# Token rows on ScalarE's DMA queue, token scales spread by a product, two parameter vectors loaded as compact rows

## The chip, the cores and the metric

One core of one Trainium2 chip runs the whole kernel as one launch. The metric is device time in microseconds (us) of one execution, as the median over several runs. TensorE does the matrix products, VectorE and ScalarE the element-wise work, GpSimd some of it too, and SyncE issues most of the transfers. In the profile these are PE (with PEld for its weight loads), DVE, ACT, POOL and SP; a "q" behind a name is the engine's instruction queue. A transfer is issued by an instruction on SP's, ACT's or POOL's queue and then runs on the core's 16 DMA engines.

## The reference, cut to what matters

2048 new tokens of one stream and 8 x 16 tokens of running streams go through one layer with shared weights. The model width is 1024.

```python
h = rmsnorm(x, norm1_g)                   # x * rsqrt(mean(x*x) + eps) * g
proj = h @ w_in                           # 1024 -> 3584
hq, hf, hi, hg, aq, ak, av = split(proj)
f = lb + (1 - lb) * sigmoid(hf)
o_h = hgrn2_scan(hq, 1 - f, hi, log(f))   # matrix state per head, chunked
o_h = rmsnorm(o_h, hg_norm_g) * silu(hg)
o_a = rmsnorm(band_attention(aq, ak, av), att_norm_g)
x = x + concat(o_h, o_a) @ w_out
x = x + relu(rmsnorm(x, norm2_g) @ w_up) ** 2 @ w_down
y = rmsnorm(x, final_norm_g)
```

The change concerns the first norm (its factor per token, here called the token scale), the norm weights `hg_norm_g` and the lower bound `lb`, which comes from `lb_param`.

## The kernel before

The 2176 tokens are 17 tiles of 128 (number 16 holds the running streams). Three phases follow one another: `phase_hgrn` (projections for the recurrence, woven with the scan), `phase_att` (projections for attention, woven with attention, and the output product) and `phase_mlp`. The first two go through the tiles in six groups, `GROUPS = [[0, 1, 16], [2, 3, 4], [5, 6, 7], [8, 9, 10], [11, 12, 13], [14, 15]]`. Every big product is three products of fp32r halves (`mm3`, L290 to L292): high times high, high times low, low times high.

**Weights.** `W` (L245 to L258) loads 512 KB pieces on SP's queue into `wraw`, which has two slots. ACT casts each to the high half (L256) and DVE subtracts to get the low half (L257), into slots for two weight blocks. A block of 256 columns serves all tiles of a group.

**Token tiles.** For each group an `HT` object makes the transposed, normed activations `hT_hi` and `hT_lo`. `load` (L175) fetches the transposed tile `xT` (512 KB, L182), multiplies it by the norm weights (L185), and gets `rb`, a 128x128 tile of token scales. `put` (L192) multiplies by the scales (L199) and splits into high and low (L201, L202). This is done for every tile twice: once in the first phase and once in the second, 34 times in all.

**Token scales.** `token_scale` (L205) fetches the tile's rows a second time, untransposed (512 KB on SP's queue, L210), into `x`, a buffer with one slot (`c.xst`). ACT squares and sums (L87), POOL turns the sum into the scale (L77, L79), and POOL's queue stores the 128 scales, 4 bytes each, in a DRAM tensor `rd` (L212). For all loads but the first three, `rb` is then read back with one DRAM row copied to all 128 partitions (L189, on SP's queue). For the first three tiles ACT spreads the scale along a row (L187) and PE turns it by a product with the identity (L197, tile `rT`).

**Small parameters.** `gain_tile` (L65) loads `hg_norm_g` as one DRAM row copied to 128 partitions (256 KB into SBUF, L68). `lower_bound` (L336) loads 512 single elements into a 128x4 tile (L343). The mask table `mf` (L588) uses the one slot of `c.xst` too.

**Order.** The program is written as generators that `weave` mixes by costs written into the code, and the token scales of the next group stand after the `f` projections of the group at hand (L405). The framework under the kernel then puts each engine's instructions in an order of its own, which is fixed before the run: an instruction that waits for nothing in that order's reckoning can stand far ahead of its place in the text. On the chip each engine and each queue works in that fixed order.

Of the kernel before, what the change touches and what calls it, by code (L numbers as in the profile page):

```python
# [8 lines left out]
F32 = mybir.dt.float32  # L9
# [3 lines left out]
AF = mybir.ActivationFunctionType  # L13
ALU = mybir.AluOpType
# [3 lines left out]
P = 128  # L18
D = 1024
KT = D // P  # L20
NPT = 16
NTT = 17
# [7 lines left out]
GROUPS = [[0, 1, 16], [2, 3, 4], [5, 6, 7], [8, 9, 10], [11, 12, 13], [14, 15]]  # L30
# [6 lines left out]
HN = KT * P * max(len(x) for x in GROUPS_M)  # L37
# [27 lines left out]
def gain_tile(c, pool, name, a):  # L65
    n = a.shape[-1]
    t = pool.tile([P, n], F32, name=name)
    c.nc.sync.dma_start(out=t, in_=a.broadcast_to([P, n]))  # L68
    return t


def rsq(c, ss, n, width, key="", r=None):
# [18 lines left out]
def rows(c, prompt, sample, t):  # L91
    return prompt[t * P:(t + 1) * P, :] if t < NPT else sample
# [56 lines left out]
class HT:  # L149
# [24 lines left out]

    def load(self, t):  # L175
        c, nc = self.c, self.c.nc
        first = t in GROUPS[0] and t not in c.r1_known
        rb = c.small.tile([P, P], F32, tag="rb", name="rb", bufs=3)
        if first:
            token_scale(c, t)  # L180
        xT = c.xin.tile([P, D], F32, tag="x", name="xT")
        nc.sync.dma_start(out=xT, in_=c.xT[t])  # L182
        xT = xT.rearrange("p (k t) -> p k t", k=KT)
        eng = nc.vector if first and t != NPT else nc.gpsimd
        eng.tensor_tensor(out=xT, in0=xT, in1=c.g1[:, :, None].broadcast_to([P, KT, P]), op=ALU.mult)  # L185
        if first:
            nc.scalar.activation(rb, c.ones, AF.Copy, scale=c.r1[:, t:t + 1])  # L187
        else:
            nc.sync.dma_start(out=rb, in_=c.rd[t:t + 1, :].broadcast_to([P, P]))  # L189
        return xT, rb, first  # L190

    def put(self, x, col):  # L192
        c, nc = self.c, self.c.nc
        xT, rb, first = x
        if first:
            ps = c.ps_tx.tile([P, 4, P], F32, tag=c.ps_tx_tag, name="rT")[:, 0, :]
            nc.tensor.matmul(ps, rb, c.ident, start=True, stop=True)  # L197
            rb = ps
        nc.vector.tensor_tensor(out=xT, in0=xT, in1=rb[:, None, :].broadcast_to([P, KT, P]), op=ALU.mult)  # L199
        h = self.hi[:, :, col]  # L200
        nc.scalar.copy(h, xT)  # L201
        nc.vector.tensor_tensor(out=self.lo[:, :, col], in0=xT, in1=h.bitcast(F32), op=ALU.subtract)  # L202


def token_scale(c, t):  # L205

    nc = c.nc
    c.r1_known.add(t)
    x = c.xst.tile([P, D], F32, tag="x", name="x")
    nc.sync.dma_start(out=x, in_=rows(c, c.x_prompt, c.x_sample, t))  # L210
    rsq(c, sumsq(c, x, D), 1, D, r=c.r1[:, t:t + 1])
    nc.gpsimd.dma_start(out=c.rd[t:t + 1, :].rearrange("o p -> p o"), in_=c.r1[:, t:t + 1])  # L212


class OT(HT):
# [111 lines left out]
def fm_cost(cs):  # L327
    return 0.01 * (cs.stop - cs.start) / PARTS
# [7 lines left out]
def lower_bound(c, pool):  # L336

    nc = c.nc
    a = pool.tile([P, 4], F32, name="lb_a")
    e = pool.tile([P, 4], F32, name="lb_e")  # L340
    c.lb = pool.tile([P, 4], F32, name="lb")
    c.lb1 = pool.tile([P, 4], F32, name="lb1")
    nc.sync.dma_start(out=a, in_=c.lb_param.rearrange("o (h p) -> p (o h)", p=P))  # L343
    mx = pool.tile([P, 4], F32, name="lb_m")
    nc.vector.tensor_copy(mx, a)
    nc.vector.tensor_tensor(out=a, in0=a, in1=mx, op=ALU.subtract)
    nc.scalar.activation(e, a, AF.Exp)
    nc.vector.reciprocal(a, e)
    nc.vector.tensor_tensor(out=e, in0=e, in1=a, op=ALU.mult)
    nc.vector.tensor_tensor(out=c.lb, in0=e, in1=e, op=ALU.subtract)  # L350
    nc.vector.tensor_scalar(out=c.lb1, in0=c.lb, scalar1=-1.0, scalar2=1.0, op0=ALU.mult, op1=ALU.add)


def hgrn_proj(c, gs, start):

    nc = c.nc
    hT = start
    GMAX = max(len(x) for x in GROUPS) * P
    flat = c.h0p.tile([P, HN], F32, tag="h_hi", name="qf")
    b = c.h0p.tile([P, HN], F32, tag="h_lo", name="bias")  # L360
    c.bias = b[:, :AH * 640].rearrange("p (h k) -> p h k", h=AH)
    c.oa = b[:, AH * 640:AH * 640 + D]
    for gi, g in enumerate(gs):
        tiles = GROUPS[gi]
        n = len(tiles) * P
        nxt = None
        g.v = [c.hv.tile([P, 512], F32, tag="v", name="v") for _ in tiles]

        def tok(w, dst, ch, sig, done, pre=None):
            for j in range(len(tiles)):  # L370
                if pre:
                    pre()
                for _, ps in proj_tm(c, w, hT, [j]):
                    if ps is None:
                        yield TM_COST
                        continue
                    d = dst[j][:, ch * WC:(ch + 1) * WC]
                    if sig:
                        sg = c.sig.tile([P, 512], F32, tag="sig", name="sig")[:, :WC]
                        nc.scalar.activation(sg, ps, AF.Sigmoid)  # L380
                        nc.gpsimd.tensor_tensor(out=sg, in0=sg, in1=c.hgain[:, ch * WC:(ch + 1) * WC], op=ALU.mult)
                        nc.vector.tensor_tensor(out=d, in0=ps, in1=sg, op=ALU.mult)  # L382
                    else:
                        nc.scalar.copy(d, ps)
                    yield TM_COST
                done.append(j)

        w = next(c.ws)
        yield from tok(w, g.v, 0, False, [], pre=hT.add)
        o = 4 * GMAX * (gi % 2)  # L390
        g.q, g.f = (flat[:, x:x + HGH * GMAX].rearrange("p (h n) -> p h n", h=HGH)[:, :, :n]
                    for x in (2 * o, 2 * o + HGH * GMAX))
        for ch in range(2):
            w = next(c.ws)
            for f, cs, ps in proj_fm(c, w, hT, n):
                if ps is None:
                    yield fm_cost(cs)
                    continue
                h = ch * 2 + f
                sg = c.sig.tile([P, 512], F32, tag="sig", name="sig")[:, :cs.stop - cs.start]  # L400
                nc.scalar.activation(sg, ps, AF.Sigmoid)  # L401
                nc.vector.tensor_scalar(out=g.f[:, h, cs], in0=sg, scalar1=c.lb1[:, h:h + 1],
                                        scalar2=c.lb[:, h:h + 1], op0=ALU.mult, op1=ALU.add)
                yield fm_cost(cs)
        for t in GROUPS[gi + 1] if gi + 1 < len(gs) else []:  # L405
            token_scale(c, t)
        if 1 <= gi <= 4:
            att_bias(c, 2 * gi - 2, 2)
        for ch in range(2):
            w = next(c.ws)  # L410
            for f, cs, ps in proj_fm(c, w, hT, n):
                if ps is None:
                    yield fm_cost(cs)
                    continue
                nc.scalar.copy(g.q[:, ch * 2 + f, cs], ps)
                yield fm_cost(cs)
        g.fq = True
        w = next(c.ws)
        yield from tok(w, g.v, 1, False, [])
        g.gate = [c.hv.tile([P, 512], F32, tag="gate", name="gate") for _ in tiles]  # L420
        for ch in range(2):
            w = next(c.ws)
            if ch:
                nxt = HT(c, GROUPS[(gi + 1) % len(gs)])
            fin = []
            for cost in tok(w, g.gate, ch, True, fin):
                if nxt and len(fin) > nxt.next:
                    nxt.add()
                    cost += 0.5
                yield cost  # L430
        g.ready = True
        hT = nxt
    yield from att_v(c, c.vt, GROUPS[0], hT)
    c.hT0 = hT
# [127 lines left out]
def phase_hgrn(c):  # L562
    tc, nc = c.tc, c.nc
    with ExitStack() as s:
        def pool(name, bufs, **k):
            return s.enter_context(tc.tile_pool(reuse_waits="tile", name=name, bufs=bufs, **k))
        cp = pool("h_const", 1)
# [9 lines left out]
        c.ps_o = pool("h_pso", 1, space=PSUM)  # L577
        c.ps_st = pool("h_psst", 1, space=PSUM)
        c.state = cp.tile([P, HGH, P], F32, name="state")
        hT = HT(c, GROUPS[0])  # L580
        hT.add()
        next(c.ws)
# [10 lines left out]
        c.qm = [cp.tile([P, 4 * 144], F32, name=f"qm{i}") for i in range(2)]  # L593
        for x in c.qm:
            nc.gpsimd.memset(x, 0.0)
        c.hgain = gain_tile(c, cp, "hgain", c.hg_g)
        gs = [Ctx() for _ in GROUPS]
        for g in gs:
            g.ready = g.fq = False
# [505 lines left out]
def hymba_kernel(ctx, tc, x_prompt, x_sample, state_hgrn, cache_k, cache_v, lb_param, norm1_g, w_in,  # L1105
# [3 lines left out]
    c = Ctx()  # L1109
# [11 lines left out]
    dram = pool("dram", 1, space=DRAM)  # L1121
    c.small = pool("small", 2)
    consts(c, const)
    c.og = dram.tile([NTT * P, D], F32, name="og") if dbg is None else dbg
    c.rd = dram.tile([NTT, P], F32, name="rd")
    c.x1 = dram.tile([NTT * P, D], F32, name="x1")
    c.sq, c.sk = (dram.tile([4, P, P], F32, name=x) for x in ("sq", "sk"))
    c.sv = dram.tile([P, 512], F32, name="sv")
# [7 lines left out]
    with ExitStack() as s:  # L1136
        c.vp0 = s.enter_context(tc.tile_pool(reuse_waits="tile", name="v0", bufs=3))
        hTp = s.enter_context(tc.tile_pool(reuse_waits="tile", name="hT", bufs=1))
        n = max(len(x) for x in GROUPS) * P
# [68 lines left out]
```

## Time and profile before

| what | value |
|---|---|
| time, median of 3 runs | 3036.85 us (3036.55 to 3037.67) |
| profiled execution, its own time | 3034.61 us |
| its span, first to last instruction | 3032.8 us |
| PE busy | 2904.2 us, 96% |
| DVE, ACT, POOL busy | 1746.6, 1103.7, 301.5 us |
| mean granted clock of TensorE | 0.984 |
| moved by DMA | 330.48 MB, mean 109 GB/s |

Busy time of PE is the time in which a matmul runs, at whatever clock was granted; a granted clock of 0.5 is 1.2 GHz and 1.0 is 2.4 GHz. The "chain that ended last" follows the work back from the last instruction to what released each step. A wait names the instruction that waited and the one that it was put down to.

### The profile page before, as it was taken

To read this page: it belongs to the slowest core of one execution; us is meant where nothing else is said; L and a number is where in the kernel's file an instruction comes from. 1 tells how busy PE (TensorE), PEld (TensorE's weight loads), DVE (VectorE), ACT (ScalarE), POOL (GpSimd) and SP (SyncE) were. 2 spreads that over 40 slices of the span, in tenths; PEclk is the share of its full clock that TensorE was granted. 3 is DMA by queue.
4 is the path that set the end of the run, shared out by engine and by line. 5 is a ranking of instruction groups with operands and counts; after the bars stand their busy time and mean duration, and the time that the engine had idled before them with its cause. 6 is when DMAs were issued, how large, how long until landed. Compare 5 with 4: busy or idle time off the path is not lost.

```text
span 3032.8 us, 47202 instructions
## 1 busy us (share of the span) xinstructions
PE 2904.2 (96%) x18902; PEld 2680.0 (88%) x18902; DVE 1746.6 (58%) x3114; ACT 1103.7 (36%) x2258; POOL 301.5 (10%) x509
## 2 busy tenths in 40 slices
PE   5789999999999999998999999999999999999998
PEld 5788999998889888988888899999999999899997
DVE  4357666675556565656555546555555555555555
ACT  3242343343544545454222323233322223322232
POOL 2221222222002020102000000000000000000000
PEclk8889999999999999999999999999999999999999
DMA  8764333343325243446532332233212122322221
GB/s 171 159 130 127 97 120 115 94 148 126 111 82 174 74 155 105 144 153 208 190 100 65 113 113 88 73 98 118 76 57 70 56 70 86 123 70 83 71 83 64
DMA packets 118796, 330.48 MB, mean 109 GB/s; under 512 B 14192, under 2 KB 42480, under 8 KB 118576
## 3 DMA queue, kind: packets, MB, share of 16 engines
q1 hardware_dynamic: 111712, 308.84, 34.0%
q0 software_dynamic: 6864, 18.63, 1.6%
q8 instruction: 148, 2.42, 0.3%
q14 instruction: 72, 0.59, 0.1%
HBM read 294.90 MB, written 32.51 MB: 108 GB/s over the span
## 4 chain that ended last, share of the span: by engine, by line
PE 81%; DMA 8%; DVE 4%; ACT 2%; issue 2%; POOL 2%; SPq 0%; ACTq 0%; POOLq 0%; DVEq 0%
PE mm L290 23%; PE mm L292 23%; PE mm L291 23%; PE ps_oT L708 3%; DMA x<-in_x_prompt 2%; PE S L679 2%; PE S L701 2%; PE ps_sc L472 2%; DMA wraw<-in_w_in 1%; DMA rd<-r 1%; ACT junk L87 1%; DVE wlo L257 1%; PE ps_sc L465 1%; PE tx L101 1%; DMA x<-x 1%
## 5 line engine op out<-in xcount | busy, mean ns | idle before, releaser
L256 ACT CAST whi<-wraw 128x512 fp32r<-128x512 f32 x816 | 497.5, 620 | 753.7 <-PE mm L292 560.8
L257 DVE TENSOR_TENSOR wlo<-wraw,whi 128x512 fp32r<-128x512 f32 x816 | 562.5, 705 | 241.8 <-ACT whi L256 238.3
L290 PE MATMUL mm<-h_hi,whi 128*128 128x384 f32 (+1 forms) x1536 | 503.2, 328 | 1.9 <-DVE h_lo L104 1.9
L292 PE MATMUL mm<-h_hi,wlo 128*128 128x384 f32 (+1 forms) x1536 | 501.4, 326 | 0.0
L291 PE MATMUL mm<-h_lo,whi 128*128 128x384 f32 (+1 forms) x1536 | 500.7, 326 | 0.0
L1081 DVE TENSOR_TENSOR y<-mm,y 128x512 f32<-128x512 f32 x544 | 373.3, 689 | 219.3 <-PE mm L292 217.6
L290 PE MATMUL mm<-whi,uh 128*128 128x512 f32 x1088 | 423.6, 389 | 2.4 <-ACT uh L1061 2.4
L292 PE MATMUL mm<-whi,ul 128*128 128x512 f32 x1088 | 424.3, 390 | 0.8 <-DVE ul L1062 0.7
L291 PE MATMUL mm<-wlo,uh 128*128 128x512 f32 x1088 | 424.0, 390 | 0.0
L290 PE MATMUL mm<-whi,hT_hi 128*128 128x256 f32 x1264 | 381.6, 302 | 42.5 <-DVE gate L382 16.2
L292 PE MATMUL mm<-whi,hT_lo 128*128 128x256 f32 x1264 | 371.5, 294 | 3.6 <-DVE hT_lo L104 2.2
L291 PE MATMUL mm<-wlo,hT_hi 128*128 128x256 f32 x1264 | 370.1, 293 | 0.0
L290 PEld LDWEIGHTS mm<-whi,hT_hi 128*128 128x128 f32 x1264 | 250.6, 198 | 55.5 <-DVE gate L382 17.7
L290 PEld LDWEIGHTS mm<-h_hi,whi 128*128 128x128 f32 x1536 | 288.4, 188 | 6.9 <-issue 3.5
L291 PEld LDWEIGHTS mm<-h_lo,whi 128*128 128x128 f32 x1536 | 288.4, 188 | 1.2
L292 PEld LDWEIGHTS mm<-h_hi,wlo 128*128 128x128 f32 x1536 | 288.4, 188 | 0.0
L290 PE MATMUL mm<-hT_hi,whi 128*128 128x384 f32 (+1 forms) x768 | 263.7, 343 | 19.8 <-ACT sig L401 13.4
L1059 DVE SCALAR_TENSOR_TENSOR u<-mm,u 128x384 f32<-128x384 f32 (+1 forms) x192 | 102.4, 533 | 279.3 <-ACT u L1058 279.3
L292 PEld LDWEIGHTS mm<-whi,hT_lo 128*128 128x128 f32 x1264 | 250.8, 198 | 8.6 <-DVE hT_lo L104 3.1
L291 PE MATMUL mm<-hT_lo,whi 128*128 128x384 f32 (+1 forms) x768 | 256.0, 333 | 0.0
L292 PE MATMUL mm<-hT_hi,wlo 128*128 128x384 f32 (+1 forms) x768 | 255.7, 333 | 0.0
L291 PEld LDWEIGHTS mm<-wlo,hT_hi 128*128 128x128 f32 x1264 | 251.1, 199 | 1.9 <-issue 1.4
(182 smaller groups left out, 4008.1 us busy)
## 6 DMA issues: line engine op xcount, KB each, us to landing
wraw<-in_w_in SPq DMA_DIRECT2D x168, 512.0 KB, 4.3
wraw<-in_w_up SPq DMA_DIRECT2D x96, 512.0 KB, 4.1
wraw<-in_w_down SPq DMA_DIRECT2D x96, 512.0 KB, 4.0
wraw<-in_w_out SPq DMA_DIRECT2D x48, 512.0 KB, 3.9
xT<-in_x_T SPq DMA_DIRECT2D x34, 512.0 KB, 4.5
og<-og SPq DMA_DIRECT2D x17, 512.0 KB, 4.0
x<-yo POOLq DMA_DIRECT2D x68, 128.0 KB, 3.3
x<-x SPq DMA_DIRECT2D x17, 512.0 KB, 5.1
```

Source lines behind the costliest of these rows:

```text
L87: nc.scalar.activation(junk[:, :n], x, AF.Square, accum_out=ss)
L256: nc.scalar.copy(hi, rw)
L257: nc.vector.tensor_tensor(out=lo, in0=rw, in1=hi.bitcast(F32), op=ALU.subtract)
L290: nc.tensor.matmul(ps, lh, rh, start=(i == 0), stop=False)
L291: nc.tensor.matmul(ps, lh, rl, start=False, stop=False)
L292: nc.tensor.matmul(ps, ll, rh, start=False, stop=(i == n - 1))
L472: nc.tensor.matmul(pc[:, h * n2:(h + 1) * n2, :], ks[:, h, :], up[:, h], start=True, stop=True)
L679: nc.tensor.matmul(S[:, bk, :n], a[es, qc], c.K[ft][es, b, kc], start=(a is q and not b), stop=(a is ql))
L701: nc.tensor.transpose(ps[:, x, :], s[:, x * P:(x + 1) * P], c.ident)
L708: nc.tensor.matmul(poT[64 * e:64 * e + 64, j, :], g.vt[i - nk + 1 + x][:, 64 * h:64 * h + 64], pts[e][:, x, :], start=(x == 0), stop=(x == ...
L1059: nc.vector.scalar_tensor_tensor(out=u2, in0=ps, scalar=0.0, in1=u2, op0=ALU.max, op1=ALU.mult)
L1081: nc.vector.tensor_tensor(out=ysl, in0=ps, in1=ysl, op=ALU.add)
```

## The change

The rows of a token tile for its scale are issued on ACT's queue instead of SP's. For group 0 all three tiles' rows are loaded at the very start, each into a part of its own of the large tile `qf` (`c.xfirst`). For later groups a generator, `token_scales`, is advanced at each finished `f` and `q` projection of the group before: one step computes the scale of the last tile loaded and issues the load of the next one. The scales stay in the SBUF tile `c.r1`: the store to `rd`, the tensor `rd` and the read back are gone, and every `load` makes `rb` with an ACT instruction and every `put` turns it with a product with the identity, as only the first three did. `hg_norm_g` is loaded as one 2 KB row and spread by a product with a row of ones and a copy from PSUM; `lb_param` is loaded as four rows of 512 bytes and transposed on PE.

```diff
+def gain_rows(c, t, a, ps_pool, tag):
+    nc = c.nc
+    n = a.shape[-1]
+    nc.sync.dma_start(out=t[0:1, :], in_=a)
+    def spread():
+        for o in range(0, n, 512):
+            ps = ps_pool.tile([P, 512], F32, tag=tag, name="grow_ps")
+            nc.tensor.matmul(ps, c.ones[0:1, :], t[0:1, o:o + 512], start=True, stop=True)
+            nc.scalar.copy(t[:, o:o + 512], ps)
+    return spread
...
     def load(self, t):
-        first = t in GROUPS[0] and t not in c.r1_known
-        rb = c.small.tile([P, P], F32, tag="rb", name="rb", bufs=3)
+        first = t not in c.r1_known
         if first:
-            token_scale(c, t)
+            token_scale(c, t, c.xfirst[t])
...
-        if first:
-            nc.scalar.activation(rb, c.ones, AF.Copy, scale=c.r1[:, t:t + 1])
-        else:
-            nc.sync.dma_start(out=rb, in_=c.rd[t:t + 1, :].broadcast_to([P, P]))
+        rb = c.small.tile([P, P], F32, tag="rb", name="rb", bufs=3)
+        nc.scalar.activation(rb, c.ones, AF.Copy, scale=c.r1[:, t:t + 1])
...
     def put(self, x, col):
-        if first:
-            ps = c.ps_tx.tile([P, 4, P], F32, tag=c.ps_tx_tag, name="rT")[:, 0, :]
-            nc.tensor.matmul(ps, rb, c.ident, start=True, stop=True)
-            rb = ps
-        nc.vector.tensor_tensor(out=xT, in0=xT, in1=rb[:, None, :].broadcast_to([P, KT, P]), op=ALU.mult)
+        ps = c.ps_tx.tile([P, 4, P], F32, tag=c.ps_tx_tag, name="rT")[:, 0, :]
+        nc.tensor.matmul(ps, rb, c.ident, start=True, stop=True)
+        nc.vector.tensor_tensor(out=xT, in0=xT, in1=ps[:, None, :].broadcast_to([P, KT, P]), op=ALU.mult)
...
-def token_scale(c, t):
+def token_scale(c, t, x):
     c.r1_known.add(t)
-    x = c.xst.tile([P, D], F32, tag="x", name="x")
-    nc.sync.dma_start(out=x, in_=rows(c, c.x_prompt, c.x_sample, t))
     rsq(c, sumsq(c, x, D), 1, D, r=c.r1[:, t:t + 1])
-    nc.gpsimd.dma_start(out=c.rd[t:t + 1, :].rearrange("o p -> p o"), in_=c.r1[:, t:t + 1])
+
+def token_scales(c, tiles):
+    x = None
+    for t in list(tiles) + [None]:
+        if x is not None:
+            token_scale(c, last, x)
+        if t is not None:
+            last, x = t, c.xst.tile([P, D], F32, tag="x", name="x")
+            c.nc.scalar.dma_start(out=x, in_=rows(c, c.x_prompt, c.x_sample, t))
+        yield
...
 def lower_bound(c, pool):
-    nc.sync.dma_start(out=a, in_=c.lb_param.rearrange("o (h p) -> p (o h)", p=P))
+    row = c.small.tile([P, P], F32, tag="rb", name="rb", bufs=3)[0:4, :]
+    nc.sync.dma_start(out=row, in_=c.lb_param.rearrange("o (h p) -> (o h) p", p=P))
+    ps = c.ps_tx.tile([P, 4, P], F32, tag=c.ps_tx_tag, name="lbT")[:, 0, :4]
+    nc.tensor.transpose(ps, row, c.ident[0:4, 0:4])
+    nc.vector.tensor_copy(a, ps)
...
 def hgrn_proj(c, gs, start):
-    flat = c.h0p.tile([P, HN], F32, tag="h_hi", name="qf")
+    flat = c.qf
...
+        scales = token_scales(c, GROUPS[gi + 1] if gi + 1 < len(gs) else [])
...
+                next(scales, None)      # after each f projection, and after each q projection
                 yield fm_cost(cs)
-        for t in GROUPS[gi + 1] if gi + 1 < len(gs) else []:
-            token_scale(c, t)
...
         g.fq = True
+        if not gi:
+            c.hgain_put()
...
 def phase_hgrn(c):
+        c.qf = c.h0p.tile([P, HN], F32, tag="h_hi", name="qf")
+        c.xfirst = {}
+        for j, t in enumerate(GROUPS[0]):
+            c.xfirst[t] = c.qf[:, j * D:(j + 1) * D]
+            nc.scalar.dma_start(out=c.xfirst[t], in_=rows(c, c.x_prompt, c.x_sample, t))
         hT = HT(c, GROUPS[0])
...
-        c.hgain = gain_tile(c, cp, "hgain", c.hg_g)
+        c.hgain = cp.tile([P, 512], F32, name="hgain")
+        c.hgain_put = gain_rows(c, c.hgain, c.hg_g, c.ps_tx, c.ps_tx_tag)
...
-    c.rd = dram.tile([NTT, P], F32, name="rd")
```

## Rows read from the trace of the kernel before

**Rows 1.** Windows of 100 us: busy time and instructions per engine, granted clock, DMA share, GB/s.
```profile
0.00:100.00 100.00, 59.40 (x294) 57.01 (x294) 37.17 (x52) 36.34 (x66) 28.33 (x54) 0.85 0.76 173
100.00:200.00 100.00, 74.88 (x507) 71.78 (x508) 51.57 (x95) 33.05 (x74) 26.00 (x41) 0.81 0.77 140
...
500.00:600.00 100.00, 99.50 (x771) 97.64 (x770) 64.50 (x130) 38.62 (x90) 25.43 (x39) 1.00 0.33 103
```

**Rows 2.** Instructions of PE by line and shape, 0 to 200 us.
```profile
L290 PE MATMUL mm<-whi,hT_hi 128*128 128x256 f32 x120 | 42.1, 351 | 28.3 <-DVE gate L382 10.5 <-ACT hT_hi L201 9.1 <-ACT qf L415 8.6
...
L290 PE MATMUL mm<-hT_hi,whi 128*128 128x384 f32 x88 | 33.4, 379 | 15.7 <-ACT sig L401 13.4 <-ACT v L384 2.3
```

**Rows 3.** Timeline of PE at either clock: start, duration, instruction.
```profile
14.78 0.41 PE L290 MATMUL mm<-whi,hT_hi 128*128 128x256 f32 x1
...
15.00 0.41 PE L291 MATMUL mm<-wlo,hT_hi 128*128 128x256 f32 x1
...
29.22 0.28 PE L292 MATMUL mm<-whi,hT_lo 128*128 128x256 f32 x1
...
29.34 0.28 PE L290 MATMUL mm<-whi,hT_hi 128*128 128x256 f32 x1
...
51.72 0.33 PE L292 MATMUL mm<-hT_hi,wlo 128*128 128x384 f32 x1
51.89 0.33 PE L290 MATMUL mm<-hT_hi,whi 128*128 128x384 f32 x1
```

**Rows 4.** Chain that ended last, 0 to 600 us: start, duration, what.
```profile
11.54 10.54 DMA x<-in_x_sample
...
49.99 11.57 DMA rd<-r
62.52 10.42 DMA wraw<-in_w_in
...
224.80 1.78 PE ps_sc L454 x16
```

**Rows 5.** Waits of SP's queue, 0 to 200 us: total, times, longest.
```profile
SPq L210 <- DMA x<-in_x_prompt: 46.1, 10, 8.5
...
SPq L189 <- DMA rd<-r: 37.1, 6, 10.8
```

**Rows 6.** Windows of 10 us, columns as in rows 1.
```profile
10.00:20.00 10.00, 6.21 (x26) 5.70 (x26) 6.85 (x7) 3.51 (x6) 3.43 (x4) 1.00 1.02 113
...
40.00:50.00 10.00, 10.00 (x60) 9.96 (x59) 4.10 (x6) 6.63 (x11) 4.14 (x7) 1.00 0.99 246
...
60.00:70.00 10.00, 4.56 (x19) 4.24 (x17) 2.66 (x3) 0.00 (x0) 0.00 (x0) 0.84 0.73 33
```

**Rows 7.** Waits of ACT, 0 to 200 us.
```profile
ACT junk L87 <- DMA x<-in_x_prompt: 63.2, 13, 12.1
```

**Rows 8.** Instructions on tile x, 0 to 200 us: count, duration (ns) min/median/max, first and last start.
```profile
L87 ACT ACTIVATE junk<-x x17: 1044/1057/1058, 4.8 to 171.5; 128x1024 bf16<-128x1024 f32 x17
L210 SPq DMA_DIRECT2D x<-in_x_prompt x16: 327/328/944, 1.2 to 163.0; - x16
...
DMA to landing us min/median/max: 3.7/8.3/11.2
```

**Rows 9.** DMA issues of the whole run: count, KB each, median us to landing.
```profile
xT<-in_x_T SPq DMA_DIRECT2D x34, 512.0 KB, 4.5
```

**Rows 10.** Read backs and the multiplication by scales, whole run, columns as in rows 8.
```profile
L189 SPq DMA_DIRECT2D rb<-rd x31: 319/327/1374, 52.8 to 1076.2; - x31
...
L199 DVE TENSOR_TENSOR xT<-xT,rb x31: 1207/1215/2918, 61.8 to 1221.5; 128x1024 f32<-128x1024 f32 x31
```

**Rows 11.** Timeline at the start: the first scale's product, the first projection product.
```profile
8.33 0.80 PE L197 MATMUL rT<-ident,rb 128*128 128x128 f32 x2 [8.33 <-ACT rb L187]
...
12.51 0.58 PE L290 MATMUL mm<-whi,hT_hi 128*128 128x256 f32 x1 [3.38 <-ACT hT_hi L201]
...
24.27 0.40 ACT L187 ACTIVATE rb<-ones,r 128x128 f32<-128x128 f32 x1
```

More of the change, by code (lines that the diff above doesn't have):

```diff
@@ L185, in load @@
         eng.tensor_tensor(out=xT, in0=xT, in1=c.g1[:, :, None].broadcast_to([P, KT, P]), op=ALU.mult)
-        if first:
-            nc.scalar.activation(rb, c.ones, AF.Copy, scale=c.r1[:, t:t + 1])
-        else:
-            nc.sync.dma_start(out=rb, in_=c.rd[t:t + 1, :].broadcast_to([P, P]))
-        return xT, rb, first
+        rb = c.small.tile([P, P], F32, tag="rb", name="rb", bufs=3)
+        nc.scalar.activation(rb, c.ones, AF.Copy, scale=c.r1[:, t:t + 1])
+        return xT, rb
     def put(self, x, col):
         c, nc = self.c, self.c.nc
-        xT, rb, first = x
-        if first:
-            ps = c.ps_tx.tile([P, 4, P], F32, tag=c.ps_tx_tag, name="rT")[:, 0, :]
-            nc.tensor.matmul(ps, rb, c.ident, start=True, stop=True)
-            rb = ps
-        nc.vector.tensor_tensor(out=xT, in0=xT, in1=rb[:, None, :].broadcast_to([P, KT, P]), op=ALU.mult)
+        xT, rb = x
+        ps = c.ps_tx.tile([P, 4, P], F32, tag=c.ps_tx_tag, name="rT")[:, 0, :]
+        nc.tensor.matmul(ps, rb, c.ident, start=True, stop=True)
+        nc.vector.tensor_tensor(out=xT, in0=xT, in1=ps[:, None, :].broadcast_to([P, KT, P]), op=ALU.mult)
         h = self.hi[:, :, col]
@@ L202, in put @@
         nc.vector.tensor_tensor(out=self.lo[:, :, col], in0=xT, in1=h.bitcast(F32), op=ALU.subtract)
-def token_scale(c, t):
-    nc = c.nc
+def token_scale(c, t, x):
     c.r1_known.add(t)
-    x = c.xst.tile([P, D], F32, tag="x", name="x")
-    nc.sync.dma_start(out=x, in_=rows(c, c.x_prompt, c.x_sample, t))
     rsq(c, sumsq(c, x, D), 1, D, r=c.r1[:, t:t + 1])
-    nc.gpsimd.dma_start(out=c.rd[t:t + 1, :].rearrange("o p -> p o"), in_=c.r1[:, t:t + 1])
+def token_scales(c, tiles):
[7 more added lines that the diff above has]
+        yield
 class OT(HT):
@@ L415, in hgrn_proj @@
                 nc.scalar.copy(g.q[:, ch * 2 + f, cs], ps)
+                next(scales, None)
                 yield fm_cost(cs)
         g.fq = True
+        if not gi:
+            c.hgain_put()
         w = next(c.ws)
```

## Prediction

> **What bounds the kernel now.** I first read the windows of busy time. From 500 us on PE is busy nearly all the time at full clock, with 99.5 of 100 us as the pattern [rows 1]; nothing but less work on PE makes that part shorter. The first 200 us are different: PE is busy for 59.4 and 74.9 us, so 65.7 us are idle, and the granted clock is 0.85 and 0.81 there [rows 1]. So I looked for what this change can win in those 200 us, and for what it costs on PE after them.
>
> How much work is in the 200 us? PE ran 801 instructions there (294 + 507) [rows 1]. By line and shape, 120 x 3 are projection products with 256 columns and 88 x 3 with 384 [rows 2]; the other 177 belong almost all to the scan. At full clock successive projection products start 0.12 us apart with 256 columns and 0.17 us with 384; at granted clock 0.5 the spacing for 256 is 0.22 [rows 3]. The scan's records cost 1.78/16 = 0.111 us each in a dense stretch [rows 4]. The work is then 360 x 0.12 + 264 x 0.17 + 177 x 0.111 = 43.2 + 44.9 + 19.6 = 107.7 us. The stage takes 200. Of the 92.3 us between, 65.7 are idle and 26.6 are busy time at the low clock.
>
> Next, what released the work. In the chain that ended last the early pieces are transfers, not products: 10.5 us for the third tile's rows, 11.6 us for the 512-byte store to `rd`, then 10.4 us for a weight piece that stood behind it [rows 4]; row after row load follows in it up to 162 us. The waits of SP's queue say why the weight piece was late: SP stood 37.1 us for the `rd` store to land before it could issue the read back (L189), and 46.1 us for the one slot of `x` (L210) [rows 5]; weight pieces are issued behind both. The windows of 10 us show that the DMA engines are not short of capacity: at 40 us they moved 246 GB/s, but at 10 us 113 and at 60 us 33 GB/s while their busy share was 1.02 and 0.73 [rows 6]. In the second of these `rb` read-backs were in flight, in the first `hgain` and `lb_a`: transfers that copy one row 128 times or take single elements fill the engines with little data.
>
> Last, ACT. It stood 63.2 us in 13 waits for an `x` tile [rows 7]. All 17 sums of squares ran between 4.8 and 171.5 us [rows 8], although the text has each group's behind projections of the group before: the framework moved them ahead. In that order ACT's casts and copies stand behind each of these waits, and PE behind them.
>
> **The change part by part.**
>
> *Start.* The rows of tiles 0, 1 and 16 are issued at once and need no slot. The first scale product starts at 8.3 us and the first projection product at 12.5 us [rows 11]; the three row loads share the DMA engines with `xT` and the first weights now, so I keep 12.5 us. The 10.5 us for tile 16's rows [rows 4] go, and `mf`, `hgain` and `lb` no longer stand in front of weights.
>
> *Store and read back.* 31 read-backs (L189) [rows 10] and 17 stores leave; with them SP's 37.1 us [rows 5] and the 11.6 + 10.4 us of the chain at 50 us [rows 4]. What is late next there is PE itself or ACT.
>
> *Row loads on ACT's queue.* SP's 46.1 us [rows 5] go. The load still needs the one slot, which ACT frees itself, so ACT's path for the 14 later tiles stays serial: issue, landing, sum. Issue is 0.33 and the sum 1.06 us [rows 8]. For the landing I have 8.3 us here as the median, among the slow transfers [rows 8], and 4.5 us as the whole run's median for a piece of the same size [rows 9]. So 14 tiles take between 14 x 5.9 = 82 and 14 x 9.7 = 136 us. I take 5.7 us, nearer to the lower end since the transfers that filled the engines are gone but weights and biases are denser: 14 x 7.1 = 99 us. Queued behind the waiting sum on ACT are casts, sigmoids and copies, and behind those PE.
>
> *How long the stage gets.* By PE alone: 11.7 us of start (12.5 less the 0.8 that PE was busy), 107.7 of work, and 5 us because the first busy us run at half clock as now (6.2 of them up to 20 us [rows 6], where the spacing, not the clock's column, shows it, and about 4 more before the spacing is 0.12 at 29.2 us [rows 3]; half of the 10 is lost): 124 us. By ACT: the first of the 14 loads can go at about 20 us (it goes at 30.7 now, and the chain there loses the 10.5 us), then 99, then the 28 us that the stage has behind its last sum (200 - 171.5): 147 us. ACT's path is the longer: 147 us, a gain of 53. With the two landings it is 130 or 184, a gain of 70 or 16. Later stages only shift, PE being full.
>
> Of the landing a rule of the Trainium skill speaks against the change. Transfers started by several engines run on the same 16 DMA engines and interleave; starting them from another queue saves only issue time (DMA: Bandwidth & Descriptors, section "Issuing engines are not separate DMA queues"). By it the new queue itself shortens no landing, and with 8.3 us the sum would be a gain of 16 for the stage instead of 53; the trace bears it out so far as it shows landings of 8.3 us in the crowd and 4.5 elsewhere, and cannot show two queues here, ACT issuing nothing now.
>
> *New work on PE.* 31 products with the identity come in. The nearest row of the same shape, 128x128 in fp32 as two records, is the scan's 2 x 0.111 = 0.22 us [rows 4]; alone and at half clock such a pair took 0.80 [rows 11]. In a dense stream the first holds: 31 x 0.22 = 6.9 us (upper bound 24.8). `hgain`'s spread has four times the columns in one product, 0.9 us. The transposed `lb` is below 0.22. All of it counts in full, for PE has no slack after 200 us: 8 us.
>
> *Costed at nothing.* 31 more ACT instructions of 0.40 us [rows 11], 12.4 us in all, hide in ACT's idle 60% (38.6 busy of 100 us in the dense stage [rows 1]); if a wait of ACT uncovers them they are 12.4 us. DVE reads the scales from PSUM instead of SBUF in the same instruction. In the second phase the product takes one of three PSUM banks of `mm` until DVE is done with it; at worst 17 x 1.2 us, the length of one multiplication [rows 10], 20 us. POOL loses 17 issues and was not the bound.
>
> *Sum.* Gain 53 - 8 = 45 us. The profiled execution took 3034.6 us (span 3032.8 and 1.8 around it): 2989.6. The median is 2.2 us above it: 2992.
>
> **The rivals.**
>
> *ACT's queue is where the wait goes (gain small).* The landing stays at 8.3 us: 16 - 8 = 8 us, 3029. For it: ACT's 63.2 us [rows 7] remain by construction, the slot still being one. Against it: the landings were long beside transfers that now leave [rows 6]. Chance 0.18, for 3012 to 3031. The rule of the Trainium skill named above would make this case.
>
> *The order changes in favour of PE (gain large).* The framework may leave the row loads further back, now that they cost ACT's time, or ACT's waits may fall under PE's work; then PE's path binds: 200 - 124 - 8 = 68, 2969. For it: two PSUM banks of products and two weight blocks stand between ACT and PE. Against it: they did not hide ACT's waits before. Chance 0.15.
>
> *Slower: PE itself waits for the scales.* Before, a late `rb` held DVE's L199; now it holds a product in PE's fixed order, and behind it the projections. Place: the 14 products of the later groups in the first phase. Price: ACT's mean wait for a tile, 63.2/13 = 4.9 us [rows 7], is what an `rb` behind such a wait is late: 14 x 4.9 = 68, so 45 - 68 = 23 us slower, 3060. It decides from 45/14 = 3.2 us per product. For it: PE's first product waited 8.3 us for exactly this [rows 11]. Against it: only group 1's three scales are computed near their use; the others are known long before. Chance 0.08.
>
> *Nothing changes* because another early wait (weights through two slots) takes over: 0.04.
>
> **How the numbers follow.** My forecast, 2992 with its own range of 2976 to 3012, has 0.55. The range of 2971 to 3028 takes in that, most of the small gain and about half of the large one. Under 0.2% (6 us) a change cannot be told from none here. Faster by more: 0.55 + 0.18 + 0.15 = 0.88; same 0.04; slower 0.08.
>
> **What would show it.** In the profile after, SP's waits for `rd` and `x` are gone and weight pieces follow one another in the first 150 us; PE's idle time in the first 200 us falls from 65.7 to about 25 and its granted clock rises; the last sum of squares comes at about 120 us instead of 171; ACT's waits for `x` stay near 14 with some 3 us each. PE's busy time of the `rT` product is about 8 us in all. I am wrong if landings on ACT's queue stay at 8 us, if `rT` shows long waits of PE, or if the sums of squares are no longer in the first 150 us.

## Result and the profile after

The changed kernel takes 3002.68 us (median of 4 runs, 2997.01 to 3009.67); the kernel before took 3036.95 beside it. The ratio is 0.9888 with a 95% interval of 0.9867 to 0.9909. The forecast was 2992 us with a range of 2971 to 3028. The time lies in the range and the direction is right; the gain is 34 us where 45 was forecast. What follows shows that the length of the first stage came out almost as worked out, in part by luck, and that the reason given for it was mostly the wrong one.

The windows of the kernel after, with the columns of [rows 1] and [rows 6]:

```profile
0.00:100.00 100.00, 79.42 (x528) 75.59 (x529) 59.06 (x96) 53.23 (x100) 31.44 (x62) 1.00 0.74 243
100.00:200.00 100.00, 94.66 (x680) 90.27 (x680) 63.75 (x124) 38.33 (x86) 19.49 (x27) 0.95 0.37 117
...
10.00:20.00 10.00, 3.24 (x9) 2.06 (x9) 7.37 (x9) 7.44 (x14) 4.30 (x5) 1.00 0.84 284
...
60.00:70.00 10.00, 10.00 (x61) 8.99 (x61) 2.58 (x4) 4.61 (x9) 0.84 (x3) 1.00 0.75 241
```

PE is idle for 200 - 79.4 - 94.7 = 25.9 us of the first 200 instead of 65.7 [rows 1], and the granted clock rose from 0.85 and 0.81 to 1.00 and 0.95. The two windows in which the DMA engines were busy with little data [rows 6] now move 284 and 241 GB/s, at busy shares of 0.84 and 0.75 (1.02 and 0.73 before).

Instructions on tile `x`, and the waits of ACT and SP's queue, 0 to 200 us, in the kernel after:

```profile
L228 ACTq DMA_DIRECT2D x<-in_x_prompt x14: 334/334/352, 25.0 to 105.7; - x14
L101 ACT ACTIVATE junk<-x x14: 1044/1057/1058, 30.8 to 112.7; 128x1024 bf16<-128x1024 f32 x14
...
DMA to landing us min/median/max: 3.5/4.5/8.0
```
```profile
ACT junk L101 <- DMA x<-in_x_prompt: 23.4, 13, 4.9
```
```profile
SPq L268 <- DVE wlo L274: 105.3, 32, 12.3
SPq L195 <- DVE hT_lo L211: 20.5, 5, 10.4
```

Rows land after 4.5 us instead of 8.3 [rows 8], the last sum of squares starts at 112.7 us instead of 171.5, ACT waits 23.4 us for rows instead of 63.2 [rows 7], and SP waits mostly for buffers that DVE frees and for 16.9 us behind weight loads; its waits for `rd` and `x` [rows 5] are gone.

A landmark gives the stage's gain: the first scan tile's output is issued at 199.07 us before and at 145.41 after, 53.7 us earlier (53 was forecast). One execution tells this only to some 5 us: a second profile of the changed kernel (E5) has 150.01 us. In the first profile the lead then shrinks: 42.6 us at the 17th scan tile (720.52 against 677.92), 38.2 at the 16th attention tile (1390.01 against 1351.79), 33.1 at the end of the span. So 21 us are given back, where the forecast had 8.

### The profile page after: what moved, and what is told of

It is laid out like the page before. It is cut to its first block, busy times and chain, and to the rows that moved or that the text cites. A ratio compares the mean times of both kernels' runs of the same rounds, so it can differ in the third digit from the quotient of the medians.

```text
span 2999.7 us, 47223 instructions
## 1 busy us (share of the span) xinstructions
PE 2905.3 (97%) x18967; PEld 2680.4 (89%) x18967; DVE 1750.2 (58%) x3115; ACT 1117.1 (37%) x2290; POOL 293.8 (10%) x492
## 4 chain that ended last, share of the span: by engine, by line
PE 71%; DVE 2%; ACT 2%; DMA 1%; issue 1%; POOL 0%; POOLq 0%; ACTq 0%; SPq 0%; DVEq 0%
PE mm L307 21%; PE mm L309 21%; PE mm L308 21%; PE ps_oT L738 3%; PE S L731 2%; PE S L709 2%; PE tx L115 1%; DMA x<-x 1%; ACT s L722 1%; ACT junk L101 0%; PE ps_os L800 0%; DVE wlo L274 0%; DVE y L125 0%; ACT whi L273 0%; POOL r L93 0%
## 5 line engine op out<-in xcount | busy, mean ns | idle before, releaser
L274 DVE TENSOR_TENSOR wlo<-wraw,whi 128x512 fp32r<-128x512 f32 x816 | 574.7, 720 | 229.7 <-ACT whi L273 222.1
```

The source lines that it names most:

```text
L274: nc.vector.tensor_tensor(out=lo, in0=rw, in1=hi.bitcast(F32), op=ALU.subtract)
```

## Experiments

Each kernel was timed against the kernel before on the same chip; the ratios are to that kernel. E1 to E4, E5 to E8 and E9 to E12 ran together on one chip each.

My account when the first four went out was that of the prediction: SP's queue stood behind waits, with weights queued behind it, and copied rows filled the DMA engines. The rival was the second queue that gives nothing.

One difference between the kernels lies at the end of the program, where POOL runs a closing instruction, DRAIN, that all engines wait for. It takes 9.75 us in every profiled kernel that issues 111 transfers on POOL's queue (the changed kernel in both its profiles, E1, E3, E4, E7, E11, E12) and 1.4 to 2.5 us in those that issue 128 (the kernel before, E2, E6, E8, E9, E10). With 111 the span ends 8.2 to 8.3 us behind the issue of the last store of results, with 128 it ends 3.2 to 3.7 us behind it. So a kernel with 111 of them is about 5 us longer for a reason that has nothing to do with the first stage. Why the number of POOL's transfers goes with that time is open.

**E1: the changed kernel, row loads on SP's queue.**

```diff
-            c.nc.scalar.dma_start(out=x, in_=rows(...))
+            c.nc.sync.dma_start(out=x, in_=rows(...))
...
-            nc.scalar.dma_start(out=c.xfirst[t], in_=rows(...))
+            nc.sync.dma_start(out=c.xfirst[t], in_=rows(...))
```

> The changed kernel with all row loads issued on SP's queue again; the slots, the order in the text and everything else stay as changed. My account (SP's queue was blocked by waits, and weights stood behind them): SP must again wait for the one slot before each of 14 loads, weights stand behind, and about 10 us of the 34 come back: near 3013 us. Rival (a second queue runs on the same 16 DMA engines and gives nothing by itself): within 3 us of the changed kernel, near 3003 us.

Measured: 2992.01 us, ratio 0.9854 (0.9840 to 0.9869). Not slower than the changed kernel but faster: its interval and that of the changed kernel's second measurement (E5, 0.9884 to 0.9919) do not touch. SP's wait for the slot was back, and cost nothing:

```profile
SPq L228 <- DMA x<-in_x_prompt: 13.7, 6, 4.0
...
SPq L228 <- ACT junk L101: 5.6, 7, 1.6
```

The waits of SP's queue, 0 to 200 us, of E1: 19.3 us behind row loads, and the first scan tile's output is issued at 140.15 us, 5 us before that of the changed kernel in its first profile and 10 before its second. My account of the row queue fell.

**E2: the changed kernel with the store and the read back.**

```diff
+    c.nc.gpsimd.dma_start(out=c.rd[t:t + 1, :].rearrange("o p -> p o"), in_=c.r1[:, t:t + 1])
...
-        nc.scalar.activation(rb, c.ones, AF.Copy, scale=c.r1[:, t:t + 1])
+        if first:
+            nc.scalar.activation(rb, c.ones, AF.Copy, scale=c.r1[:, t:t + 1])
+        else:
+            nc.sync.dma_start(out=rb, in_=c.rd[t:t + 1, :].broadcast_to([P, P]))
...
```

> The changed kernel with the store of the scales to DRAM and the broadcast read back on SP's queue (31 of them), so only the first three tiles use the product. My account: SP's wait for the store returns (37 us before), the clogged DMA engines too, while 31 products of 0.22 us leave PE: near 3020 us. Rival (the round trip was hidden and the freed queue did all): 7 us faster than the changed kernel, near 2996 us.

Measured: 3043.09 us, ratio 1.0025 (1.0015 to 1.0035). All of the gain is gone, not half of it. Rows on ACT's queue and compact parameter rows together bring nothing while the round trip is there.

**E3: the changed kernel with the wide parameter loads.** `gain_tile` for `hg_norm_g` and the element-wise load for `lb_param` are put back.

> The changed kernel with the norm weights loaded as 128 copies of one row and the lower bound as single elements, as before. My account: at 10 to 20 us these filled the DMA engines at 113 GB/s, so the start loses 3 to 8 us: 3006 to 3011 us. Rival (nothing waits for them, they are used late): 3003 us within 3.

Measured: 2993.86 us, ratio 0.9870 (0.9854 to 0.9886). The wide loads cost nothing: by the ratios it is 5 to 9 us faster than the changed kernel, though the intervals still overlap. Neither account had that.

**E4: the scales alone.** The kernel before, with a product for every tile and without `rd`.

```diff
-        if first:
-            nc.scalar.activation(rb, c.ones, AF.Copy, scale=c.r1[:, t:t + 1])
-        else:
-            nc.sync.dma_start(out=rb, in_=c.rd[t:t + 1, :].broadcast_to([P, P]))
-        return xT, rb, first
+        nc.scalar.activation(rb, c.ones, AF.Copy, scale=c.r1[:, t:t + 1])
+        return xT, rb, True
...
-    nc.gpsimd.dma_start(out=c.rd[t:t + 1, :].rearrange("o p -> p o"), in_=c.r1[:, t:t + 1])
...
```

> The kernel before with one part of the change alone: no store and read back of scales, a product for every tile. Rows stay on SP's queue in program order as before, gains as before. My account: SP's 37 us of waits go and the row loads' waits stay, PE has 8 us more work: about half of the whole gain, near 3018 us. Rival (the row queue is the main part): 3037 us or slower by the 8 us of products, 3045.

Measured: 2990.69 us, ratio 0.9855 (0.9841 to 0.9869): more than the whole gain, from one part of three (the interval touches that of the changed kernel's first measurement, not that of its second, E5). So, with E2, the round trip through `rd` is the cause. It has three pieces, and the next runs take them one at a time: the stores, the copied rows, and SP's wait.

**E5: the changed kernel once more**, beside the next three.

> The changed kernel once more, beside the next three on one chip and for comparison with the first four. If rows on ACT's queue, loaded into places of their own at the start, cost something of themselves: a ratio near 0.989 as first measured, some 8 us slower than the scales alone (0.9855). If the first measurement differed by chip only: 0.986.

Measured: 3004.40 us, ratio 0.9901 (0.9884 to 0.9919). The first measurement holds; the other two parts cost something of themselves.

**E6: the stores alone.** The changed kernel plus the tensor `rd` and the store to it, the first line of E2's edit; nobody reads `rd`.

> The changed kernel with the 17 stores of 128 scales of 4 bytes each back on POOL's queue, read by nobody. If the small stores themselves fill the DMA engines or hold POOL: 15 to 35 us slower than the changed kernel. If the wait of SP for them is what cost, or the read backs: the changed kernel's time within 3 us.

Measured: 3043.94 us, ratio 1.0026 (1.0014 to 1.0039). Seventeen stores of 512 bytes each, for which nobody waits, take all of the gain: 39.5 us more than E5, beyond the 15 to 35 expected. Windows of 2 us of E6 (columns as in [rows 1]); stores are issued at 42.7 and 48.5 us:

```profile
42.00:44.00 2.00, 1.70 (x7) 1.70 (x8) 1.72 (x3) 2.00 (x5) 1.00 (x2) 0.79 1.00 372
44.00:46.00 2.00, 2.00 (x8) 2.00 (x8) 2.00 (x4) 0.62 (x2) 0.00 (x0) 0.50 2.52 213
46.00:48.00 2.00, 2.00 (x12) 2.00 (x10) 1.32 (x4) 1.90 (x3) 0.59 (x2) 0.86 0.31 18
48.00:50.00 2.00, 1.24 (x7) 0.92 (x7) 0.83 (x4) 1.41 (x3) 0.80 (x2) 1.00 0.63 18
50.00:52.00 2.00, 2.00 (x14) 2.00 (x13) 0.42 (x1) 0.00 (x0) 0.00 (x0) 1.00 0.41 20
52.00:54.00 2.00, 2.00 (x13) 2.00 (x13) 0.00 (x0) 0.00 (x0) 0.00 (x0) 1.00 0.78 309
```

and the same stretch of the changed kernel:

```profile
46.00:48.00 2.00, 2.00 (x14) 2.00 (x13) 1.27 (x4) 1.15 (x2) 0.51 (x2) 1.00 0.75 227
48.00:50.00 2.00, 2.00 (x12) 1.68 (x11) 1.36 (x3) 1.82 (x4) 0.23 (x1) 1.00 0.86 311
50.00:52.00 2.00, 2.00 (x13) 2.00 (x12) 1.08 (x2) 0.72 (x2) 0.00 (x0) 1.00 0.71 221
```

With the stores, the rate falls from 372 to 18 GB/s for three windows while 31 to 63% of the engines' time counts as busy; without them it stays above 220. Row loads land after 7.1 us in E6 (median) and weights after 9.3, where the changed kernel has 4.5 and 4.0. ACT's wait for rows is 68.9 us (63.2 before the change [rows 7]).

A count over the first 200 us makes the kernels comparable: windows of 2 us with a busy share of at least 0.25 and under 60 GB/s.

| kernel | such windows of 100 | ratio |
|---|---|---|
| before | 22 | 1 |
| changed | 1 | 0.9888 |
| E6 stores only | 22 | 1.0026 |
| E7 copied rows only | 2 | 0.9891 |
| E8 stores, one row read | 24 | 1.0071 |
| E9 row-wise store | 1 | 0.9809 |
| E10 short loads | 3 | 0.9865 |
| E11 stores on ACT's queue | 44 | 1.0106 |

**E7: the copied rows alone.**

```diff
+        if not first and not hasattr(c, "K"):
+            rbx = c.oa[:, P * (t % 3):P * (t % 3) + P]
+            nc.sync.dma_start(out=rbx, in_=c.x_prompt[0:1, 0:P].broadcast_to([P, P]))
```

> The changed kernel with the 14 read backs of the first phase back on SP's queue, but as 128 copies of a row of the input that waits for no store, into a place that nobody reads. If the copied rows clog the DMA engines (as the 33 GB/s at 60 us before suggested): 15 to 30 us slower than the changed kernel. If only the wait cost: within 3 us of it.

Measured: 3000.57 us, ratio 0.9891 (0.9875 to 0.9907): no cost. 17 such loads were issued between 9.5 and 69.3 us (three for the second phase's first group come on top of the 14).

**E8: the stores and SP's wait for them**, with a read back of one row.

```diff
+    c.nc.gpsimd.dma_start(out=c.rd[t:t + 1, :].rearrange("o p -> p o"), in_=c.r1[:, t:t + 1])
...
+        if not first and not hasattr(c, "K"):
+            rbx = c.oa[0:1, P * (t % 3):P * (t % 3) + P]
+            nc.sync.dma_start(out=rbx, in_=c.rd[t:t + 1, :])
```

> The changed kernel with the 17 stores and, in the first phase, 14 read backs on SP's queue of the one row that was stored, 512 bytes into one partition instead of 128 copies, used by nobody. SP must wait for each store, but little data moves. If SP's wait, with weights queued behind it, is the cost: 20 to 35 us slower than the changed kernel. If the copied rows are: within 5 us of it.

Measured: 3056.35 us, ratio 1.0071 (1.0055 to 1.0087). The waits of SP's queue, 0 to 200 us:

```profile
SPq L203 <- DMA rd<-r: 115.9, 13, 13.6
```

SP waits three times as long for stores as in the kernel before (37.1 us [rows 5]), and that costs 12 us more than the stores without any wait (E6). The wait is the smaller part.

**E9: the kernel before, with the store row-wise.** Everything else of the kernel before stays: rows on SP's queue, the copied read back, SP's wait, wide parameters.

```diff
-    nc.gpsimd.dma_start(out=c.rd[t:t + 1, :].rearrange("o p -> p o"), in_=c.r1[:, t:t + 1])
+    ps = c.ps_tx.tile([P, 4, P], F32, tag=c.ps_tx_tag, name="rrow")[0:1, 0, :]
+    nc.tensor.matmul(ps, c.r1[:, t:t + 1], c.ident, start=True, stop=True)
+    row = c.small.tile([P, P], F32, tag="rb", name="rb", bufs=3)[0:1, :]
+    nc.scalar.copy(row, ps)
+    nc.gpsimd.dma_start(out=c.rd[t:t + 1, :], in_=row)
```

> The kernel before with one change: each tile's 128 scales are first turned into a row (a product with the identity, a copy by ACT) and stored as one run of 512 bytes instead of 128 runs of 4 bytes. The read back as 128 copies, SP's wait for the store, the rows on SP's queue and the wide gains all stay. If the 4-byte runs of the store are the whole cost: near 2992 us, as the scales alone. If the waits of SP for the store or the copied rows carry part of it: between 3005 and 3037 us.

Measured: 2978.70 us, ratio 0.9809 (0.9791 to 0.9826), the fastest of all. The waits of SP's queue and the transfers, both 0 to 200 us:

```profile
SPq L210 <- DMA x<-in_x_prompt: 15.0, 8, 5.1
...
SPq L189 <- DMA rd<-rb: 6.4, 2, 3.6
```
```profile
x<-in_x_prompt SPq DMA_DIRECT2D x16, 512.0 KB, 4.4
...
rb<-rd SPq DMA_DIRECT2D x6, 64.0 KB, 3.0
...
hgain<-in_hg_norm_g SPq DMA_DIRECT2D x1, 256.0 KB, 4.8
...
rd<-rb POOLq DMA_DIRECT2D x9, 0.5 KB, 3.9
```

and the same transfers in the kernel before, 0 to 200 us:

```profile
rb<-rd SPq DMA_DIRECT2D x9, 64.0 KB, 7.2
...
rd<-r POOLq DMA_DIRECT2D x17, 0.5 KB, 11.6
hgain<-in_hg_norm_g SPq DMA_DIRECT2D x1, 256.0 KB, 14.1
```

The same 512 bytes land after 3.9 us instead of 11.6, the copied rows after 3.0 instead of 7.2 and the wide norm weights after 4.8 instead of 14.1: the last two had looked slow only beside the stores. SP's wait for the store shrinks from 37.1 us [rows 5] to 6.4, being mostly a consequence, not a cause. The order changed too: only 9 of the 17 stores fall into the first 200 us, against 17 before. They leave 1 window of the count, against 22. By the ratios E9 is some 14 us faster than E4; 5 of them are the end of the program, and the rest is not settled.

**E10: short loads in place of the stores.**

```diff
+    s = c.small.tile([P, 1], F32, tag="ssl", name="ssl", bufs=1)
+    c.nc.gpsimd.tensor_copy(s, c.r1[:, t:t + 1])
+    c.nc.gpsimd.dma_start(out=s, in_=c.x_prompt[0:1, 0:P].rearrange("o p -> p o"))
```

> The changed kernel with 17 loads of 128 runs of 4 bytes from the input on POOL's queue at the places of the former stores, into a tile that nobody reads. If short runs cost the engines the same in either direction: near 3044 us, like the stores. If it is writing short runs to DRAM: within 4 us of the changed kernel, 3003.

Measured: 2994.88 us, ratio 0.9865 (0.9848 to 0.9882). Runs of 4 bytes read from DRAM cost nothing that shows here. By the ratios the kernel is 7 to 11 us faster than the changed one, of which 5 are the end of the program. Issuing these loads holds POOL for 0.61 us each, just as the stores of E6 do, so POOL's issuing is not what the stores cost.

**E11: the stores on ACT's queue.**

```diff
-    rsq(c, sumsq(c, x, D), 1, D, r=c.r1[:, t:t + 1])
+    ss = sumsq(c, x, D)
+    c.nc.scalar.dma_start(out=c.rd[t:t + 1, :].rearrange("o p -> p o"), in_=ss)
+    rsq(c, ss, 1, D, r=c.r1[:, t:t + 1])
...
```

> The changed kernel with 17 stores of 128 runs of 4 bytes (the sums of squares, read by nobody) issued on ACT's queue instead of POOL's. If the runs themselves hold the DMA engines, whoever issues them: near 3044 us, like the stores on POOL's queue. If it is the way in which POOL's queue makes its transfers: within 6 us of the changed kernel, 3003.

Measured: 3067.95 us, ratio 1.0106 (1.0090 to 1.0121). The queue that issues them is no cure; here it is worse, with 44 windows of the count instead of 22 (16 of the 17 stores fall into these 200 us). Of the 24 us between E11 and E6, 5 are the end of the program. Such a store lands after 8.1 us (median), and rows behind it on that queue after 11.1.

**E12: two places for rows**, on top of E4.

```diff
-    x = c.xst.tile([P, D], F32, tag="x", name="x")
+    x = c.oa if hasattr(c, "oa") and t % 2 else c.xst.tile([P, D], F32, tag="x", name="x")
```

> The scales on chip alone, with a second place for the row loads (an unused stretch of the bias tile for odd tiles), so that a load no longer waits for the last sum. If ACT's serial path over one slot (23 us of waits left) still sets the first stage: 4 to 10 us faster than the scales alone, 2982 to 2987 us. If weights and PE set it by now: 2991 us within 3.

Measured: 2984.68 us, ratio 0.9833 (0.9815 to 0.9851). Some 7 us less than E4 by the ratios, but the intervals overlap; with rows landing after 4.4 us in E4 the one slot is at most a small bound.

## Why the prediction was right or wrong, point by point

**What bounds the kernel: right.** The loss was in the first 200 us, and PE's 65.7 idle us and low clock there were what could be won.

**Start: 12.5 us kept, too early.** The first projection product starts at 17.7 us. ACT's order there has the cast of the first weights, which waits until 11.6 us for their landing, in front of the second tile's sum and the first `rb` (13.2 us). With the rows on SP's queue (E1) all three sums stand ahead of that cast, `rb` comes at 8.8 and the product at 13.2.

**Store and read back: right in what it gives, wrong in why. This is the step that failed.** It put the gain down to SP's 37.1 us of waiting and to copied rows that fill the DMA engines. The copied rows cost nothing (E7), the wait is the smaller part (E8 against E6), and the stores alone undo everything (E6). I had read the two slow windows of [rows 6] by the transfers issued in them, which were loads of copied rows and single elements. The stores of the scales were in flight too, issued on POOL's queue, and I counted them as half a KB. E9 shows it from the other side: with the same bytes in one run, the rest of the kernel before needs no change. The Trainium skill has the hint: below 512 bytes per transfer a DMA engine reads, modifies and writes (DMA: Bandwidth & Descriptors, section "Specifications"). That such stores are dear agrees with the traces (18 GB/s for all traffic after one); that reading and modifying is what makes them so, no run here shows. The short loads of E10, which write their runs of 4 bytes to SBUF, have no such cost. No run separates the length of the runs from their number, or from the fact that all 128 of a store go to the same 512 bytes of DRAM.

**Row loads on ACT's queue: wrong.** SP's 46.1 us in front of the `x` slot were a symptom of late landings too. The queue alone brings nothing; the changed kernel is 10 to 14 us slower than E1 (0.9888 and 0.9901 against 0.9854). Part of it is the start, 4.5 us by the products above. The rest is not settled. The rule that I weighed against the change, that another queue uses the same engines, was right about the queue; the landing still fell to 4.5 us because of the stores, so its case (3029 us) did not come.

**The landing and the stage: the number right, in part by luck.** 5.7 us was taken for the landing and 4.5 measured; the stage gained 53.7 us for 53 (49.1 in E5's profile). Errors in its terms cancel: the first of the 14 loads went at 25.0 us (20 was taken), the loads and sums then took 89 us (99), and 33 us passed from the start of the last sum to the first scan tile (28). Nor do the runs bear out that ACT's path sets the stage's end: in E1 the last sum starts at 120.0 us, 7 us later than in the changed kernel, and the first scan tile comes 5 us earlier.

**New work on PE: within noise, and not the loss.** 34 scale products ran (68 records of 0.27 us that overlap). Between the 17th scan tile and the 16th attention tile, where 17 of them fall, the lead shrank by 4.4 us after the change (42.6 to 38.2), but in E9, which has no product there, by 4.8 as well (59.4 to 54.6).

**The sum: 45 forecast, 33 in the profile.** The term that was mis-sized is what is given back later. Of 21 us, 11.1 went by the 17th scan tile, 5.9 of it in one stretch between two scan tiles. There PE waited for DVE, and behind the short gap its granted clock was halved, as these windows of the changed kernel show:

```profile
343.00:348.00 5.00, 2.76 (x27) 2.38 (x25) 5.00 (x6) 2.06 (x5) 1.90 (x1) 0.99 0.74 272
348.00:353.00 5.00, 5.00 (x29) 4.82 (x28) 3.75 (x8) 1.28 (x3) 0.00 (x0) 0.50 0.36 110
```

PE is idle for 2.24 us while DVE is busy throughout, and in the next 5 us the clock is 0.50. Each edit makes the framework order the engines anew, and between the first and the 17th scan tile E3 gave back 2.2 us, E4 5.5 and E5 10.6; I have no rule for it. Another 5 us are the end of the program, and that is a term that the prediction put at nothing ("POOL loses 17 issues and was not the bound"): the last five stores of results take 14.6 us to issue in both, and the span ends 3.3 us behind that in the kernel before (3032.8 - 3014.9 - 14.6) and 8.3 in the changed one (2999.7 - 2976.8 - 14.6). POOL's closing DRAIN takes 2.48 us in the first and 9.75 in the second, where it ends 5 us after SP is through (2998.9 against 2993.9 us). With 17 transfers put back on POOL's queue, stores (E6) or loads (E10), it is 2.48 again. The other 4.4 us went between the 17th scan tile and the 16th attention tile.

**The rivals.** The small gain did not come, the landing being short. The large gain did not either: PE still stood idle for 25.9 us of the first 200, and lost part of the lead later. PE did wait for a scale once for 13.6 us, at the start (8.3 before [rows 11]), but hardly at the later ones: the slower case did not come.

## What to carry to other kernels

When windows show the DMA engines busy at a few GB/s, look for what is being written, however few bytes it is: 17 stores of 128 runs of 4 bytes cost this kernel as much as the whole change won. Turn a column into a row on chip before it goes to DRAM. Waits for a slow landing (a blocked queue, a full slot) spread far from their cause, and only runs that put back one piece at a time told the cause from its symptoms.

## What the runs showed of the hardware that was not expected

A store of 128 runs of 4 bytes to DRAM holds back the other queues' transfers, whichever of two queues issues it: 22 slow windows of 2 us for 17 stores from POOL's queue (E6), 2.6 us per store, and 44 for 16 stores from ACT's (E11), 5.5 us per store. Loads of such runs (E10) and loads of one 512-byte row copied 128 times (E7) did not. A gap of 2.24 us on PE, after some 80 us at full clock, was followed by about 6 us at half clock (0.50 in each window of 2 us from 348 to 354 us). POOL's closing DRAIN took 9.75 us in the eight profiles with 111 transfers on POOL's queue, and 1.4 to 2.5 us in the six with 128.
